# A softmax router on one core: TensorE's loop entered in the middle, and a new order of the last steps

## The chip, the core and the metric

The kernel runs on one core of a Trainium2 chip. The time is the device time of one execution in microseconds (us), the median of several runs. The profile's span is a little shorter than that time: it reaches from the first to the last instruction of one profiled execution. The engines are TensorE (PE, with its weight loads, PEld, listed apart), VectorE (DVE), ScalarE (ACT), GpSimd (POOL) and SyncE (SP).

## The reference

```python
batch, seq, dim = 16, 512, 1024
num_loras = 8
x: (16, 512, 1024) float32, router_weights: (1024, 8) float32

logits = np.matmul(x, router_weights)
exp_logits = np.exp(logits - np.max(logits, axis=-1, keepdims=True))
return (exp_logits / np.sum(exp_logits, axis=-1, keepdims=True)).astype(np.float32)
```

There are 8192 rows of 1024 numbers. Each row gives eight logits and a softmax over those eight. x is 33.6 MB, the result 0.26 MB: the kernel reads much and computes little.

## The kernel before

The 8192 rows are cut into 64 row blocks (J = 64) of 128 rows, one row to a partition. Block j is `xa[:, j, :]`. For each block TensorE turns the eight 128 x 128 pieces of x (so that the long dimension lies on the partitions), VectorE copies five of the turned pieces from PSUM to SBUF and ScalarE the other three, and TensorE multiplies them with the weights. The turned pieces lie in two sets of buffers, for even and for odd blocks. The softmax is done for groups of eight blocks on VectorE and ScalarE, and for the last three blocks (ALONE) apart.

```python
    LOADS = [4] * 13 + [2, 2, 2] + [1] * 5      # blocks in each load: all but the last block
    PIECES = [4, 2, 2]                          # the last block comes in three loads
    G, SKIP = 8, 3
    TRIPS = 31
    ALONE = 3
    NG = (J - ALONE + SKIP) // G
    starts = [max(0, G * g - SKIP) for g in range(NG)]
    ends = [G * (g + 1) - SKIP for g in range(NG)]
    DONE = ends[-2]
    # ...
    VN, SN = 5, 3                               # pieces copied by VectorE, by ScalarE
```

So the groups end with blocks 4, 12, ..., 60, and blocks 61, 62 and 63 stand alone. The first load goes through float32 and a cast on ScalarE; all others are issued by GpSimd in one sequence, and DMA writes them to SBUF as bfloat16:

```python
    for i, r in enumerate(LOADS):
        if i:
            nc.gpsimd.dma_start(
                out=xa[:, first[i]:first[i] + r, :], in_=x_rows[:, first[i]:first[i] + r, :]
            ).then_inc(s_ld[i], 16)
    # ... (at i == 2 the identity matrix and the filler are made)
    for i, n in enumerate(PIECES):
        c = slice(cols[i] * P, (cols[i] + n) * P)
        nc.gpsimd.dma_start(out=xa[:, J - 1, c], in_=x_rows[:, J - 1, c]).then_inc(s_z[i], 16)
```

SyncE tells TensorE what has landed. A product of block j waits for three counts on `s_c[j % 2]`: VectorE's copy, ScalarE's copy, and SyncE's count, which says that block j + 2 has landed. So the transposes of block j + 2, which come right behind, need no wait of their own. At the end SyncE issues the two stores:

```python
    for j in range(J - 2):
        sp.wait_ge(s_tv, j + 1)
        if j + 2 < LOADS[0]:
            sp.wait_ge(s_cast, j + 3)
        elif j + 2 in first:
            sp.wait_ge(s_ld[first.index(j + 2)], 16)
        sp.sem_inc(s_c[j % 2], 1)
    sp.wait_ge(s_z[0], 16)
    sp.wait_ge(s_out, NG - 1)
    sp.dma_start(out=out_rows[:, 0:DONE, :], in_=outv[:, 0:DONE, :]).then_inc(s_st[0], 16)
    sp.wait_ge(s_out, NG + 1)
    sp.dma_start(out=out_rows[:, DONE:J, :], in_=outv[:, DONE:J, :]).then_inc(s_st[1], 16)
```

TensorE's work is a loop of 31 trips, two blocks each. The addresses are kept in registers. `fill()` is a matmul on constant data that nobody reads: it keeps TensorE busy.

```python
    def multiply(b, dst, want=3):
        for c in range(KO):
            if c == 0:
                pe.wait_ge(s_c[b], want).then_inc(s_c[b], -want)
            # ... one 128x128 by 128x8 matmul
            if c == KO - 1:
                m.then_inc(s_p, 1)

    nc.br("rows_loop", engines=only_pe)
    with nc.body("rows_loop", valid_engines=only_pe):
        loop_turn(1)          # transposes of an odd block
        fill()
        fill()
        multiply(0, None)     # product of the even block before it
        loop_turn(0)          # transposes of the next even block
        multiply(1, None)
        pe.br_lt(r_x[0], left_of(TRIPS - 1), on_true="rows_loop", on_false="rows_done")
    nc.switch_bb("rows_done")

    # behind the loop: blocks 62 and 63
    turn_piece(0)             # waits for s_z[0], turns four pieces of block 63
    turn_piece(1)
    multiply((J - 2) % 2, alone[1], want=2)
    turn_piece(2)
    # ... product of block 63 in three parts, each behind the copy of its pieces
```

ScalarE and VectorE, with what they do last (`peak`, `diff`, `total`, `recip`, `scale` are the five VectorE steps of a group: maximum, subtraction, sum, reciprocal, product; `power` is ScalarE's exp between the second and the third; `low_alone` and `power_alone` are maximum and exp of one block that stands alone):

```python
    # ScalarE
    for j in range(J - 2):
        act_copy(j)
        if j == 1:
            cast(1)
        if j - 1 in ends[:-1]:
            power(ends.index(j - 1))
    power(NG - 1)
    power_alone(0)
    act_copy(J - 2)
    act.wait_ge(s_zt[0], 1)
    act.copy(xTz[0], z_bank[0]).then_inc(s_zc[0], 1)
    power_alone(1)
    power_alone(2)

    # VectorE
    # ... dve_copy(j) and the groups before the last, one step after each copy
    later = group(NG - 1)
    later.pop(0)()            # peak
    later.pop(0)()            # diff
    low_alone(0)
    dve_copy(J - 2)
    later.pop(0)()            # total
    dve_piece(1)
    dve_piece(2)
    low_alone(1)
    low_alone(2)
    for f in later:           # recip, scale
        f()
    dve.wait_ge(s_e3, ALONE)
    # ... sum, reciprocal and product of the blocks that stand alone
```

Of the kernel before, what the change touches and what calls it, by code (L numbers as in the profile page):

```python
# [11 lines left out]
def kernel(  # L12
# [6 lines left out]
    nc = tc.nc  # L19
    P = 128  # L20
    B, S, D = x.shape
    D2, N = router_weights.shape
# [3 lines left out]
    J = M // P  # L26
# [12 lines left out]

    LOADS = [4] * 13 + [2, 2, 2] + [1] * 5  # L40
    PIECES = [4, 2, 2]
    G, SKIP = 8, 3
    TRIPS = 31
    LOOP_T = 2 * TRIPS
    ALONE = 3
    NG = (J - ALONE + SKIP) // G
    starts = [max(0, G * g - SKIP) for g in range(NG)]
    ends = [G * (g + 1) - SKIP for g in range(NG)]
    DONE = ends[-2]
    assert sum(LOADS) == J - 1 and sum(PIECES) == KO and ends[-1] == J - ALONE  # L50
    VN, SN = 5, 3
# [20 lines left out]
    w_bf = sb("w_bf", [P, KO, N], bf16)  # L72
# [4 lines left out]
    xTz = [sb(f"xTz{i}", [P, n, P], bf16) for i, n in enumerate(PIECES)]  # L77
# [4 lines left out]
    inv = [sb(f"inv{i}", [P, G, 1], fp32) for i in range(2)]  # L82
    low = sb("low", [P, ALONE], fp32)
    ev3 = sb("ev3", [P, ALONE, N], fp32)
    sum3 = sb("sum3", [P, ALONE, 1], fp32)
    inv3 = sb("inv3", [P, ALONE, 1], fp32)


    LG_AT = 0x2000000
    lg = ps("lg", [P, 2, G, 64], fp32)  # L90
    ptv = [ps(f"ptv{i}", [P, 8, P], bf16) for i in range(2)]
    pts = [ps(f"pts{i}", [P, 8, P], bf16) for i in range(2)]
    spare = ps("spare", [P, 512], fp32)
    extra = ps("extra", [P, 8, 64], fp32)

    sem = tc.alloc_semaphore
# [4 lines left out]
    s_ld = [sem(f"s_ld{i}") for i in range(len(LOADS))]  # L101
    s_z = [sem(f"s_z{i}") for i in range(len(PIECES))]
    s_cast = sem("s_cast")
# [7 lines left out]
    s_tv = sem("s_tv")  # L111
    s_ts = sem("s_ts")
    s_c = [sem(f"s_c{i}") for i in range(2)]
    s_zt = [sem(f"s_zt{i}") for i in range(len(PIECES))]
    s_zc = [sem(f"s_zc{i}") for i in range(len(PIECES))]
    s_p = sem("s_p")
# [7 lines left out]
    first = [sum(LOADS[:i]) for i in range(len(LOADS))]  # L124
    cols = [sum(PIECES[:i]) for i in range(len(PIECES))]
# [19 lines left out]

    sp = nc.sync

    for j in range(J - 2):
        sp.wait_ge(s_tv, j + 1)
        if j + 2 < LOADS[0]:  # L150
            sp.wait_ge(s_cast, j + 3)
        elif j + 2 in first:
            sp.wait_ge(s_ld[first.index(j + 2)], 16)
        sp.sem_inc(s_c[j % 2], 1)
    sp.wait_ge(s_z[0], 16)
    sp.wait_ge(s_out, NG - 1)
    sp.dma_start(out=out_rows[:, 0:DONE, :], in_=outv[:, 0:DONE, :]).then_inc(s_st[0], 16)
# [19 lines left out]
    for i, n in enumerate(PIECES):  # L177
        c = slice(cols[i] * P, (cols[i] + n) * P)
# [5 lines left out]
    pe = nc.tensor  # L184
    r_x = [pe.alloc_register(f"rx{c}") for c in range(KO)]
# [22 lines left out]
    def loop_turn(b):  # L208

        for c in range(KO):  # L210
            t = again(
                turn_like,
                ins=(turn_like.ins[0], at([[J * D, P], [1, P]], xa, r_x[c])),
                outs=(pe.lower_ap(turn_ap(b, c), opt=False),),
            )
            if c == VN - 1:
                t.then_inc(s_tv, 1)
            if c == KO - 1:
                t.then_inc(s_ts, 1)
        pe.reg_add(r_l, r_l, 256)  # L220
        for c in range(KO):
            if c == KO // 2:
                pe.reg_alu(r_l, r_l, -4097, ALU.bitwise_and)
            pe.reg_add(r_x[c], r_x[c], D * 2)
# [7 lines left out]
                t.then_inc(s_ts, 1)  # L232
        return t

    def multiply(b, dst, want=3):

        for c in range(KO):
            if c == 0:
                pe.wait_ge(s_c[b], want).then_inc(s_c[b], -want)  # L239
            if dst is None:  # L240
                m = again(
                    mult_like,
                    ins=(
                        pe.lower_ap(w_bf[:, c, :], opt=False),
                        pe.lower_ap(chunk(b, c), opt=False, for_matmul_weights=True),
                    ),
                    outs=(at([[2 * G * 64, P], [1, N]], lg, r_l),),
                    start_tensor_calc=(c == 0),
                    stop_tensor_calc=(c == KO - 1),
                )  # L250
            else:
                m = pe.matmul(  # L252
                    dst, lhsT=chunk(b, c), rhs=w_bf[:, c, :],
                    start=(c == 0), stop=(c == KO - 1),
                )
            if c == KO - 1:
                m.then_inc(s_p, 1)

    def fill():
        return pe.matmul(spare, lhsT=filler[:, 0:P], rhs=filler, start=True, stop=True)  # L260
# [17 lines left out]
    def left_of(i):  # L278

        return X_AT + D * 2 * (2 * i + 3) + (P - 1) * 2  # L280

    only_pe = OrderedEngineSet([pe.engine])
    nc.br("rows_loop", engines=only_pe)
    with nc.body("rows_loop", valid_engines=only_pe):
        loop_turn(1)
        fill()
        fill()
        multiply(0, None)
        loop_turn(0)
        multiply(1, None)  # L290
        pe.br_lt(r_x[0], left_of(TRIPS - 1), on_true="rows_loop", on_false="rows_done")
    nc.switch_bb("rows_done")


    alone = [lg[:, NG % 2, 0, 0:N], extra[:, 0, 0:N], spare[:, 0:N]]
    z_bank = [pts[1][:, 0:PIECES[0], :], ptv[1][:, 0:PIECES[1], :], ptv[0][:, 0:PIECES[2], :]]
    Z_ORDER = (0, 1, 2)
    def turn_piece(i):
        pe.wait_ge(s_z[i], 16)
        for c in range(PIECES[i]):  # L300
            k = (cols[i] + c) * P
            t = pe.transpose(z_bank[i][:, c, :], xa[:, J - 1, k:k + P], identity)  # L302
        t.then_inc(s_zt[i], 1)

    turn_piece(0)
    turn_piece(1)
    multiply((J - 2) % 2, alone[1], want=2)
    turn_piece(2)
    todo = [(i, c) for i in Z_ORDER for c in range(PIECES[i])]
    for k, (i, c) in enumerate(todo):  # L310
        if c == 0:
            pe.wait_ge(s_zc[i], 1)
        m = pe.matmul(  # L313
            alone[2], lhsT=xTz[i][:, c, :], rhs=w_bf[:, cols[i] + c, :],
            start=(k == 0), stop=(k == KO - 1),
        )
    m.then_inc(s_p, 1)
# [14 lines left out]
    def power_alone(k):  # L332
        act.wait_ge(s_low, k + 1)
        act.activation(
            ev3[:, k, :], alone[k], func=Exp, bias=low[:, k:k + 1]
        ).then_inc(s_e3, 1)

    def act_copy(j):
        act.wait_ge(s_ts, j + 1)
        act.copy(xTs[j % 2], pts[j % 2][:, 0:SN, :]).then_inc(s_c[j % 2], 1)  # L340

    cast(0)
    for j in range(J - 2):
        act_copy(j)
        if j == 1:
            cast(1)
        if j - 1 in ends[:-1]:
            power(ends.index(j - 1))
    power(NG - 1)
    power_alone(0)  # L350
    act_copy(J - 2)
    act.wait_ge(s_zt[0], 1)
    act.copy(xTz[0], z_bank[0]).then_inc(s_zc[0], 1)
    power_alone(1)
    power_alone(2)


    dve = nc.vector
# [5 lines left out]
    def dve_copy(j):  # L364
        dve.wait_ge(s_tv, j + 1)
        dve.tensor_copy(out=xTv[j % 2], in_=ptv[j % 2][:, 0:VN, :]).then_inc(s_c[j % 2], 1)  # L366

    def group(g):
        b, n = g % 2, ends[g] - starts[g]
        rows = lg[:, b, G - n:G, 0:N]  # L370

        def peak():
            dve.wait_ge(s_p, ends[g])
            dve.reduce_max(mx[b][:, 0:n, 0], rows, axis=X).then_inc(s_d, 1)  # L374

        def diff():
            dve.wait_ge(s_d, 3 * g + 1)
            dve.tensor_tensor(  # L378
                out=ex[b][:, 0:n, :], in0=rows, in1=mx[b][:, 0:n, :].broadcast_to([P, n, N]),
                op=ALU.subtract,  # L380
            ).then_inc(s_ex, 1)

        def total():
            dve.wait_ge(s_ev, g + 1)
            dve.reduce_sum(ssum[b][:, 0:n, 0], ev[b][:, 0:n, :], axis=X).then_inc(s_d, 1)

        def recip():
            dve.wait_ge(s_d, 3 * g + 2)
            dve.reciprocal(inv[b][:, 0:n, :], ssum[b][:, 0:n, :]).then_inc(s_d, 1)  # L389

        def scale():
            dve.wait_ge(s_d, 3 * g + 3)
            dve.tensor_tensor(  # L393
                out=outv[:, starts[g]:ends[g], :], in0=ev[b][:, 0:n, :],
                in1=inv[b][:, 0:n, :].broadcast_to([P, n, N]), op=ALU.mult,
            ).then_inc(s_out, 1)

        return [peak, diff, total, recip, scale]

    def low_alone(k):  # L400
        dve.wait_ge(s_p, J - ALONE + k + 1)
        dve.reduce_max(  # L402
            low[:, k:k + 1], alone[k], axis=X, negate=True
        ).then_inc(s_low, 1)
# [3 lines left out]
        dve.tensor_copy(out=xTz[i], in_=z_bank[i]).then_inc(s_zc[i], 1)  # L408

    later = []  # L410
    for j in range(J - 2):
        dve_copy(j)
        if j in ends[:-1]:
            later += group(ends.index(j))
        if later:
            later.pop(0)()
    assert not later
    later = group(NG - 1)
    later.pop(0)()
    later.pop(0)()  # L420
    low_alone(0)
    dve_copy(J - 2)
    later.pop(0)()
    dve_piece(1)
    dve_piece(2)
    low_alone(1)
    low_alone(2)
    for f in later:
        f()
    dve.wait_ge(s_e3, ALONE)  # L430
    dve.reduce_sum(sum3[:, :, 0], ev3, axis=X).then_inc(s_d, 1)  # L431
    dve.wait_ge(s_d, 3 * (NG) + 1)
# [35 lines left out]
```

## Time and profile before

| what | before |
|---|---|
| device time, median of 3 | 87.9 us (87.88 to 87.9) |
| span of the profiled execution | 86.2 us |
| TensorE busy (matmuls) | 61.3 us, 71% |
| TensorE busy (weight loads) | 49.0 us, 57% |
| VectorE busy | 38.9 us, 45% |
| ScalarE busy | 37.9 us, 44% |
| GpSimd busy | 13.4 us, 16% |
| granted TensorE clock | 1.000 |

In the lines of the profile, "L273" is a line of the program. L260 is the line of the loop's products and of the fills, L273 that of the loop's transposes, L252 the product behind the loop, L302 the transposes of block 63, L313 its products, L366 and L340 the copies by VectorE and ScalarE, L408 and L353 those of block 63's pieces, L374 to L393 the group's softmax, L402 and L334 the maximum and exp of a block alone. A line of the timeline gives the start in us, the duration from first to last of the merged instructions in us, engine, operation, out<-in, count, and in brackets the idle time before and what ended it. Matmul ends are modelled, and a matmul overlaps the next. In a line of a window stand the window, its length, the busy time of PE, PEld, DVE, ACT and POOL (with counts), the granted clock, the busy share of the DMA engines, and the GB/s that they wrote. A line of waits names who waited for whom: us in total, times, longest.

### The profile page before, as it was taken

What the parts mean: (1) busy time and instruction counts of PE and PEld (TensorE: products, weight loads), DVE (VectorE), ACT (ScalarE), POOL (GpSimd) and SP (SyncE); (2) the same over time, 40 slices, a digit from 0 to 9 for tenths busy, and PEclk for the clock granted to TensorE, in tenths of its full rate; (3) what the DMA queues carried; (4) which work ended last, traced back from release to release, by engine and by line L of the source; (5) the groups of instructions that cost most, each with busy time, mean ns of one, the idle gap of its engine ahead of it and who ended that gap; (6) DMA issues with size and microseconds to landing.
All of it is one profiled execution on the core that took longest, in us unless ns stands there. A gap on an engine that the chain in (4) does not pass through costs nothing. (4 is left out here: it accounts for less than half of the span.)

```text
span 86.2 us, 2819 instructions
## 1 busy us (share of the span) xinstructions
PE 61.3 (71%) x1096; PEld 49.0 (57%) x1096; DVE 38.9 (45%) x113; ACT 37.9 (44%) x80; POOL 13.4 (16%) x30
## 2 busy tenths in 40 slices
PE   0051869999594949769493968859494999897940
PEld 0040827887482828466481837657381888675630
DVE  0020214676272634636172544726074557553652
ACT  0049396465262444526062443615154446544460
POOL 0489999700000000000000000000000000000000
PEclk9999999999999999999999999999999999999999
DMA  2999999999999999999999999999999999999720
GB/s 57 373 426 300 202 224 202 224 202 236 190 236 198 232 205 221 217 213 224 202 232 198 232 198 232 202 228 213 213 221 198 213 213 204 208 209 206 120 77 21
DMA packets 3906, 18.14 MB, mean 210 GB/s; under 512 B 568, under 2 KB 1080, under 8 KB 2112
## 3 DMA queue, kind: packets, MB, share of 16 engines
q0 software_dynamic: 3312, 15.73, 89.4%
q1 hardware_dynamic: 576, 2.36, 7.1%
q10 hardware_dynamic: 16, 0.03, 0.2%
q14 instruction: 2, 0.02, 0.0%
HBM read 33.59 MB, written 0.26 MB: 393 GB/s over the span
## 5 line engine op out<-in xcount | busy, mean ns | idle before, releaser
L366 DVE COPY xTv<-ptv 128x640 bf16<-128x640 bf16 x63 | 31.0, 492 | 36.3 <-PE ptv L273 32.1
L340 ACT COPY xTs<-pts 128x384 bf16<-128x384 bf16 x63 | 30.2, 479 | 38.9 <-PE pts L273 37.6
L273 PE MATMUL ptv<-identity,x_all 128*128 128x128 bf16 x311 | 27.9, 220 | 2.1 <-ACT x_all L325 2.1
L260 PEld LDWEIGHTS lg<-w_bf,xTv 128*128 128x128 bf16 x310 | 14.5, 96 | 25.1 <-issue 21.0
L260 PE MATMUL lg<-w_bf,xTv 128*128 128x8 bf16 x310 | 16.7, 167 | 14.0 <-PEq L239 13.8
L273 PE MATMUL pts<-identity,x_all 128*128 128x128 bf16 x186 | 20.7, 220 | 0.0
L273 PEld LDWEIGHTS ptv<-identity,x_all 128*128 (+1 forms) x311 | 18.2, 97 | 2.8 <-issue 2.6
L260 PE MATMUL spare<-filler 128*128 128x512 bf16 x63 | 19.5, 391 | 0.0
L260 PE MATMUL lg<-w_bf,xTs 128*128 128x8 bf16 x186 | 13.4, 166 | 0.0
L273 PEld LDWEIGHTS pts<-identity,x_all 128*128 x186 | 13.1, 99 | 0.0
L166 POOL DMA_DIRECT2D x_all<-in_x_dram x20 | 10.7, 612 | 2.8 <-POOLq L143 2.8
L260 PEld LDWEIGHTS lg<-w_bf,xTs 128*128 128x128 bf16 x186 | 9.0, 96 | 0.0
L260 PEld LDWEIGHTS spare<-filler 128*128 128x128 bf16 x63 | 5.0, 99 | 0.0
L267 PE MATMUL extra<-ident,w 8*128 8x8 f32 x8 | 1.0, 251 | 5.3 <-PEq L265 5.3
L325 ACT CAST x_all<-x_f 128x1024 bf16<-128x1024 f32 x4 | 4.0, 1044 | 0.0
L267 PEld LDWEIGHTS extra<-ident,w 8*128 8x128 f32 x8 | 0.9, 196 | 5.3 <-issue 5.3
L325 ACT ACT_TABLE_LOAD x1 | 1.3, 1283 | 5.5 <-ACTq L323 5.5
L360 DVE CAST identity<-ident 128x128 bf16<-128x128 f32 x1 | 0.5, 519 | 5.3 <-POOL ident L172 5.3
L374 DVE TENSOR_REDUCE mx<-lg 128x8 f32<-128x64 f32 (+1 forms) x8 | 1.8, 222 | 2.4 <-PE lg L260 2.4
L330 ACT ACTIVATE ev<-ex 128x64 f32<-128x64 f32 (+1 forms) x8 | 2.0, 254 | 0.8 <-DVE ex L378 0.7
L179 POOL DMA_DIRECT2D x_all<-in_x_dram x3 | 1.7, 696 | 0.0
L393 DVE TENSOR_TENSOR outv<-ev,inv 128x64 f32<-128x64 f32 (+1 forms) x8 | 1.7, 213 | 0.0
(36 smaller groups left out, 14.8 us busy)
## 6 DMA issues: line engine op xcount, KB each, us to landing
x_all<-in_x_dram POOLq DMA_DIRECT2D x12, 1024.0 KB, 32.1
x_f<-in_x_dram SPq DMA_DIRECT2D x2, 1024.0 KB, 6.2
x_all<-in_x_dram POOLq DMA_DIRECT2D x3, 512.0 KB, 60.1
x_all<-in_x_dram POOLq DMA_DIRECT2D x5, 256.0 KB, 64.2
out_dram<-outv SPq DMA_DIRECT2D x1, 212.0 KB, 1.9
x_all<-in_x_dram POOLq DMA_DIRECT2D x1, 128.0 KB, 65.8
x_all<-in_x_dram POOLq DMA_DIRECT2D x2, 64.0 KB, 65.6
out_dram<-outv SPq DMA_DIRECT2D x1, 44.0 KB, 1.5
```

What stands on the lines that cost most here:

```text
L166: nc.gpsimd.dma_start(out=xa[:, first[i]:first[i] + r, :], in_=x_rows[:, first[i]:first[i] + r, :]).then_inc(s_ld[i], 16)
L179: nc.gpsimd.dma_start(out=xa[:, J - 1, c], in_=x_rows[:, J - 1, c]).then_inc(s_z[i], 16)
L260: return pe.matmul(spare, lhsT=filler[:, 0:P], rhs=filler, start=True, stop=True)
L267: t = pe.transpose(w_ps[:, n, :], w8[:, :, n], ident[0:KO, 0:KO])
L273: turn_like = pe.transpose(turn_ap(0, 0), xa[:, 0, 0:P], identity).ins
L325: act.copy(xa[:, k, :], x_f32[:, k, :]).then_inc(s_cast, 1)
L330: act.activation(ev[g % 2][:, 0:n, :], ex[g % 2][:, 0:n, :], func=Exp).then_inc(s_ev, 1)
L340: act.copy(xTs[j % 2], pts[j % 2][:, 0:SN, :]).then_inc(s_c[j % 2], 1)
L360: dve.tensor_copy(out=identity, in_=ident).then_inc(s_idb, 1)
L366: dve.tensor_copy(out=xTv[j % 2], in_=ptv[j % 2][:, 0:VN, :]).then_inc(s_c[j % 2], 1)
L374: dve.reduce_max(mx[b][:, 0:n, 0], rows, axis=X).then_inc(s_d, 1)
L393: dve.tensor_tensor(out=outv[:, starts[g]:ends[g], :], in0=ev[b][:, 0:n, :], in1=inv[b][:, 0:n, :].broadcast_to([P, n, N]), op=ALU.mult,). ...
```

## The change

The loop's body is cut into two blocks, `rows_multiply` and `rows_turn`, and is entered at the second. Each trip now ends after the transposes of an even block, so that the last odd block's product (block 61) comes behind the loop with its own, fixed address. The fills move to just before the odd block's product. The product of an even block now waits for its two copies alone (want=2); a new count, `s_in`, tells TensorE that the next even block has landed, and it is waited for just before that block's transposes. Odd blocks keep the old wait (want=3). SyncE raises `s_in` for even blocks without waiting for TensorE first.

The groups end one block earlier (SKIP 4: they end with blocks 3, 11, ..., 59), and four blocks stand alone. The last steps of VectorE and ScalarE are put in a new order: the copies of blocks 61 and 62 come ahead of the exps of the blocks that stand alone, and the group's last steps are spread between the copies.

The purpose is that TensorE need not wait for data before a product which doesn't use it, and that little softmax work stands between the last blocks' landings and the last store.

```diff
-    G, SKIP = 8, 3
+    G, SKIP = 8, 4
-    ALONE = 3
+    ALONE = 4
+    s_in = sem("s_in")

-    for j in range(J - 2):
-        sp.wait_ge(s_tv, j + 1)
-        if j + 2 < LOADS[0]:
-            sp.wait_ge(s_cast, j + 3)
-        elif j + 2 in first:
-            sp.wait_ge(s_ld[first.index(j + 2)], 16)
-        sp.sem_inc(s_c[j % 2], 1)
+    for j in range(2, J - 1):
+        if j % 2:
+            sp.wait_ge(s_tv, j - 1)
+        if j < LOADS[0]:
+            sp.wait_ge(s_cast, j + 1)
+        elif j in first:
+            sp.wait_ge(s_ld[first.index(j)], 16)
+        sp.sem_inc(s_c[1] if j % 2 else s_in, 1)

-    def multiply(b, dst, want=3):
+    def multiply(b, dst, want=2):

-    nc.br("rows_loop", engines=only_pe)
-    with nc.body("rows_loop", valid_engines=only_pe):
-        loop_turn(1)
+    nc.br("rows_turn", engines=only_pe)
+    with nc.body("rows_multiply", valid_engines=only_pe):
         fill()
         fill()
+        multiply(1, None, want=3)
+        pe.br("rows_turn")
+    with nc.body("rows_turn", valid_engines=only_pe):
+        loop_turn(1)
         multiply(0, None)
+        pe.wait_ge(s_in, 1).then_inc(s_in, -1)
         loop_turn(0)
-        multiply(1, None)
-        pe.br_lt(r_x[0], left_of(TRIPS - 1), on_true="rows_loop", on_false="rows_done")
+        pe.br_lt(r_x[0], left_of(TRIPS - 1), on_true="rows_multiply", on_false="rows_done")

+    multiply((J - 3) % 2, alone[1])
     turn_piece(0)
     turn_piece(1)
-    multiply((J - 2) % 2, alone[1], want=2)
+    multiply((J - 2) % 2, alone[2])
     turn_piece(2)

     # ScalarE
-    for j in range(J - 2):
+    for j in range(J - 3):
         act_copy(j)
     # ...
     power(NG - 1)
-    power_alone(0)
+    act_copy(J - 3)
     act_copy(J - 2)
     act.wait_ge(s_zt[0], 1)
     act.copy(xTz[0], z_bank[0]).then_inc(s_zc[0], 1)
-    power_alone(1)
-    power_alone(2)
+    for k in range(ALONE):
+        power_alone(k)

     # VectorE
-    for j in range(J - 2):
+    for j in range(J - 3):
         dve_copy(j)
     # ...
-    later = group(NG - 1)
-    later.pop(0)()
-    later.pop(0)()
+    peak, diff, total, recip, scale = group(NG - 1)
+    peak()
+    diff()
+    dve_copy(J - 3)
+    total()
     low_alone(0)
     dve_copy(J - 2)
-    later.pop(0)()
+    recip()
+    low_alone(1)
     dve_piece(1)
     dve_piece(2)
-    low_alone(1)
     low_alone(2)
-    for f in later:
-        f()
+    low_alone(3)
+    scale()
```

(The buffers in which the four blocks alone have their logits are listed anew; that is left out here.)

More of the change, by code (lines that the diff above doesn't have):

```diff
@@ L282 @@
     only_pe = OrderedEngineSet([pe.engine])
-    nc.br("rows_loop", engines=only_pe)
-    with nc.body("rows_loop", valid_engines=only_pe):
-        loop_turn(1)
+    nc.br("rows_turn", engines=only_pe)
+    with nc.body("rows_multiply", valid_engines=only_pe):
         fill()
         fill()
+        multiply(1, None, want=3)
+        pe.br("rows_turn")
+    with nc.body("rows_turn", valid_engines=only_pe):
+        loop_turn(1)
         multiply(0, None)
+        pe.wait_ge(s_in, 1).then_inc(s_in, -1)
         loop_turn(0)
-        multiply(1, None)
-        pe.br_lt(r_x[0], left_of(TRIPS - 1), on_true="rows_loop", on_false="rows_done")
+        pe.br_lt(r_x[0], left_of(TRIPS - 1), on_true="rows_multiply", on_false="rows_done")
     nc.switch_bb("rows_done")
-    alone = [lg[:, NG % 2, 0, 0:N], extra[:, 0, 0:N], spare[:, 0:N]]
+    alone = [lg[:, NG % 2, 0, 0:N], extra[:, 0, 0:N], spare[:, 0:N], lg[:, 1 - NG % 2, 0, 0:N]]
     z_bank = [pts[1][:, 0:PIECES[0], :], ptv[1][:, 0:PIECES[1], :], ptv[0][:, 0:PIECES[2], :]]
@@ L313 @@
         m = pe.matmul(
-            alone[2], lhsT=xTz[i][:, c, :], rhs=w_bf[:, cols[i] + c, :],
+            alone[3], lhsT=xTz[i][:, c, :], rhs=w_bf[:, cols[i] + c, :],
             start=(k == 0), stop=(k == KO - 1),
```

## The prediction

> **What bounds the kernel now.** I read the page first, then SyncE's waits, then DMA in short windows around the end, then the last ten microseconds of the timeline. In the page, the rows of slices and of queues say what sets the pace:
>
> ```profile
> PE   0051869999594949769493968859494999897940
> ...
> DMA  2999999999999999999999999999999999999720
> ...
> q0 software_dynamic: 3312, 15.73, 89.4%
> ...
> HBM read 33.59 MB, written 0.26 MB: 393 GB/s over the span
> ```
>
> DMA is full from the second slice to the 37th, TensorE is not. The 33.6 MB of x come in at a fixed pace: every load is issued by GpSimd by 16.7 us, with no wait on any other engine, so no edit of the compute can move a landing. SyncE, which passes the landings on to TensorE, mostly waits for data:
>
> ```profile
> SPq L154 <- DMA x_all<-in_x_dram: 40.8, 15, 3.6
> SPq L154 <- PE ptv L273: 23.9, 30, 1.7
> ```
>
> In a burst one trip of TensorE's loop (two row blocks) takes 1.73 us (transposes of an even block start at 70.38 and again at 72.11). Four row blocks arrive in about 4.9 us (the waits after the fills end at 61.84 and 66.73), so two arrive in 2.44 us. TensorE has 0.7 us to spare per trip and is back to waiting for data by 74.08. What counts is therefore what lies behind the last loads. The windows of the end show them stop:
>
> ```profile
> 79.80:80.40 0.60, 0.60 (x8) 0.22 (x6) 0.49 (x1) 0.34 (x1) 0.00 (x0) 1.00 1.30 190
> 80.40:81.00 0.60, 0.60 (x17) 0.60 (x17) 0.23 (x1) 0.14 (x1) 0.00 (x0) 1.00 0.99 127
> 81.00:81.60 0.60, 0.60 (x18) 0.54 (x14) 0.43 (x3) 0.26 (x2) 0.00 (x0) 1.00 0.04 4
> ```
>
> The last number is GB/s: 127, then 4. The semaphores follow: the last one-block load is issued at 14.5 us and lands 65.7 us later, so block 62 is there at 80.2; the three pieces of block 63 are issued from 15.0 to 16.0 and land after 65.5 to 65.8 us, so at 80.8, about 81.2 and 81.6. But the span ends at 86.2. The 4.6 us in between are the tail, and the timeline shows who holds it up:
>
> ```profile
> 79.06 0.20 PEld L260 LDWEIGHTS lg<-w_bf,xTv 128*128 128x128 bf16 x5 [0.59 <-issue]
> ...
> 79.40 0.45 PE L273 MATMUL ptv<-identity,x_all 128*128 128x128 bf16 x5
> ...
> 79.86 0.59 PE L260 MATMUL spare<-filler 128*128 128x512 bf16 x2
> ...
> 80.34 0.20 PEld L260 LDWEIGHTS lg<-w_bf,xTv 128*128 128x128 bf16 x5 [0.38 <-issue]
> ...
> 80.57 0.44 PE L273 MATMUL ptv<-identity,x_all 128*128 128x128 bf16 x5
> ...
> 80.75 0.23 DVE L374 TENSOR_REDUCE mx<-lg 128x8 f32<-128x64 f32 x1 [0.36 <-PE lg L260]
> ...
> 81.48 0.48 DVE L366 COPY xTv<-ptv 128x640 bf16<-128x640 bf16 x1
> ...
> 81.76 0.47 ACT L340 COPY xTs<-pts 128x384 bf16<-128x384 bf16 x1
> ...
> 82.34 0.20 PEld L252 LDWEIGHTS extra<-w_bf,xTv 128*128 128x128 bf16 x5 [0.81 <-issue]
> ...
> 82.55 0.12 PEld L302 LDWEIGHTS ptv<-identity,x_all 128*128 128x128 bf16 x2
> ...
> 82.89 0.29 DVE L408 COPY xTz<-ptv 128x256 bf16<-128x256 bf16 x1 [0.60 <-PE ptv L302]
> ...
> 83.48 0.17 DVE L402 TENSOR_REDUCE low<-spare 128x1 f32<-128x8 f32 x1 [0.23 <-PE spare L313]
> ...
> 84.61 0.34 SPq L159 DMA_DIRECT2D out_dram<-outv  x1
> ```
>
> From above: product of block 59 (starts once block 61 has landed), transposes of block 61, the two fills, product of 60, transposes of 62 at 80.57. Then the copies of 62 out of PSUM at 81.48 and 81.76, late because VectorE and ScalarE first do the softmax of the last group. The 0.81 us in which TensorE then has nothing to do ends with those copies; only then come the product of 62 and the last piece's transposes at 82.55, a microsecond after that piece landed.
>
> [...] after a product that TensorE had waited for, the next transposes start 0.18 us after the start of its second part (76.73 to 76.91), against 0.08 us where TensorE's queue was full (62.61 to 62.69), so 0.1 us, and nothing when the queue is full. [...] here the exp at 81.59 lasts 0.27 and the next operation starts at 81.76, an overlap of 0.10, so each further exp adds about 0.17.
>
> **The change part by part.** (1) The loop. Order of work in a trip stays the same, cut elsewhere; the fills move from behind the odd block's transposes to behind the even block's. An even block's product no longer waits for the landing of the block two ahead; its transposes have that wait (s_in). Added per trip: one branch and one wait, about 0.1 us when visible, 31 times 0.1 = 3.1 us in all, but inside 31 times 0.7 us of spare time: zero on the path. At the end it matters. The product of 59 still waits for block 61 (79.06), and block 61's transposes stay at 79.40. The product of 60 follows directly, at 79.85 instead of 80.34. The transposes of 62 wait for their landing, 80.2 plus the 0.1 us of the hand-over by SyncE; with the 0.03 us from weight load to matmul they start at 80.36 instead of 80.57: 0.21 us earlier.
>
> (2) The groups end with block 59. VectorE's maximum needs the product of 59, over at 79.44, so it runs at 79.5 and not at 80.75, the subtraction at 79.75, ScalarE's exp at 80.0 to 80.25. All of it now lies in the wait for block 62. Block 61's copies come then (79.98 and 80.27), ready before TensorE wants them after 62's transposes. Its product goes at about 80.95 (before 81.01).
>
> (3) The copies of 62. VectorE can read 0.49 us after the first transpose starts (79.40 to 79.89 for block 61), ScalarE after 0.66 (79.40 to 80.06). Before: ready at 81.06 and 81.23, done at 81.48 and 81.76, so held up by 0.42 and 0.53 us. After: 80.36 + 0.49 = 80.85 and 80.36 + 0.66 = 81.02, with both engines free (VectorE is through with sum and the first maximum at about 80.9). ScalarE's, the later one, gains 81.76 - 81.02 = 0.74 us. The product of 62 follows 0.58 us behind it (81.76 to 82.34): 81.60.
>
> (4) From there the steps are those of before: pieces 0 and 1 are transposed before (landed at 80.8 and 81.2), last piece's transposes 0.21 later at 81.81 (landed at 81.6, so 0.2 us in hand), its copy at 82.89 - 0.74 = 82.15, the last maximum at 82.74, its exp, sum, reciprocal, product and the store's issue at 84.61 - 0.74 = 83.87. Piece 0's copy on ScalarE starts at 81.6 and ends at 82.2, in time for its four products.
>
> (5) Added behind it: one more maximum of 0.17 us (in VectorE's wait), one more exp of 0.17 us (ScalarE is through with the first three at about 82.9, as the last maximum ends), and 32 elements instead of 24 in the last three VectorE operations: the multiply of 64 took 0.23 and of 24 took 0.18 us, so 8 elements are 0.01 us, three times 0.03 us. The store carries 48 KB and not 44: from 1.9 us for 212 KB and 1.5 for 44, 0.01 us. Sum: -0.74 + 0.03 + 0.01 = -0.70 us, and 87.9 - 0.7 = 87.2 us.
>
> **Rivals.** (a) The loop becomes slower by its two branches, its extra wait and the shifted fills, and TensorE comes late to the last blocks. Against it: 0.7 us to spare in each trip. What can show is one branch of 0.1 us at the end: 87.3. [...] (b) The last piece's landing becomes the bound, since only 0.2 us are left: if it moves by 0.3 us, 0.1 us of the gain goes, 87.3. For it speaks that DMA shares grow towards the end (1.30 in a window). (c) The new order blocks an engine: VectorE's sum waits for the group's exp ahead of copy 62, and ScalarE's four exps all come after piece 0's copy. In my times the first has 0.6 us in hand, the second ends just in time; 0.2 us of queueing there makes 87.4. (d) Only the fills and the early product help, and the softmax's move is neutral, as ScalarE is loaded either way: -0.2 us, 87.7.
>
> **Range and chances.** If nothing behind the last transposes gets shorter, the gain is at most the distance from the last landing (81.6) to those transposes before (82.55): 0.95 us, so about 86.9 is the floor. With (b) to (d) there is still a gain, to 87.3 to 87.7. I take 87.2, range 86.9 to 87.6. Two per cent is 1.76 us: twice what the tail can give, so faster by 2% is nearly excluded (0.02). Slower by 2% needs a loop that loses over 0.7 us in each trip (0.03). Within 2%: 0.95.
>
> **What would show it.** Right: loads stop at the same 81 us; no fill between the transposes of 61 and the product of 60; transposes of 62 at 80.3 to 80.4; the last group's maximum near 79.5; copies of 62 at about 80.9 and 81.0; product of 62 near 81.6; last store issued near 83.9; span 85.5. Wrong: TensorE still busy with earlier blocks when block 62 lands (rival a), TensorE idle before the last piece's transposes (b), or a gap ended by VectorE's maxima or ScalarE's exps between the last product and the sum (c).

## The result and the profile after

The changed kernel takes 87.11 us (86.98 to 87.25, 4 runs) where before takes 87.9 (4 runs beside it): a ratio of 0.9904, 95% interval 0.9881 to 0.9927. In a second comparison (run 5 below) the same pair gave 0.988 (0.9857 to 0.9903), 87.06 against 88.17.

The same rows of the page, now of the changed kernel:

```profile
PE   0052639999998986959496895959597799999860
...
DMA  3899999999999999999999999999999999999920
...
q0 software_dynamic: 3312, 15.73, 89.9%
...
HBM read 33.59 MB, written 0.26 MB: 395 GB/s over the span
```

DMA has not changed in the body: it is full from the second slice on, the same bytes come in at the same pace (395 GB/s over the span, before 393). TensorE's row does differ in the first quarter, where its clock came up later (at 18.3 us, before at 11.7; see run 4): there the trace's records of the granted clock begin, at 1.0, and a matmul of a transpose takes 311 to 314 ns in the median ahead of that moment and 217 to 219 behind it. Ahead of it no clock is on record, and the page counts that as 1.000. SyncE still waits most for data, if less than before (35.1 us where it was 40.8). Its waits for TensorE's transposes are fewer (18 where there were 30), as the even blocks no longer have one, though longer in sum (29.0 us where it was 23.9):

```profile
SPq L157 <- DMA x_all<-in_x_dram: 35.1, 17, 3.0
SPq L157 <- PE ptv L276: 29.0, 18, 2.8
```

In the three windows at the end (last number: GB/s) the loads stop at the same place, a little later:

```profile
79.80:80.40 0.60, 0.44 (x13) 0.35 (x10) 0.56 (x3) 0.25 (x2) 0.00 (x0) 1.00 1.25 197
80.40:81.00 0.60, 0.48 (x8) 0.46 (x8) 0.34 (x4) 0.37 (x2) 0.00 (x0) 1.00 1.30 171
81.00:81.60 0.60, 0.59 (x16) 0.50 (x14) 0.60 (x3) 0.44 (x1) 0.00 (x0) 1.00 0.24 30
```

In the trace's record of landings the last piece of block 63 arrives at 81.69 us after the start of the span, before the change at 81.53. Over all profiled runs of this study it lies between 81.53 and 81.93, in either kernel, so this is scatter from run to run. The timeline of the tail, to be read beside that of before (lines have moved: L276 for L273, L263 for L260, L255 for L252, L348 and L374 for the copies, L416 and L361 for those of block 63):

```profile
79.22 0.20 PEld L263 LDWEIGHTS lg<-w_bf,xTv 128*128 128x128 bf16 x5 [0.42 <-issue]
...
79.45 0.44 PE L276 MATMUL ptv<-identity,x_all 128*128 128x128 bf16 x5
...
79.63 0.23 DVE L382 TENSOR_REDUCE mx<-lg 128x8 f32<-128x64 f32 x1 [0.65 <-PE lg L263]
...
79.84 0.23 PEld L263 LDWEIGHTS lg<-w_bf,xTv 128*128 128x128 bf16 x5
...
80.15 0.26 ACT L338 ACTIVATE ev<-ex 128x64 f32<-128x64 f32 x1 [1.02 <-DVE ex L386]
...
80.52 0.44 PE L276 MATMUL ptv<-identity,x_all 128*128 128x128 bf16 x5 [0.28 <-PEq L295]
...
80.99 0.49 DVE L374 COPY xTv<-ptv 128x640 bf16<-128x640 bf16 x1 [0.26 <-PE ptv L276]
...
81.16 0.48 ACT L348 COPY xTs<-pts 128x384 bf16<-128x384 bf16 x1 [0.39 <-PE pts L276]
...
81.75 0.20 PEld L255 LDWEIGHTS spare<-w_bf,xTv 128*128 128x128 bf16 x5
81.75 0.59 ACT L361 COPY xTz<-pts 128x512 bf16<-128x512 bf16 x1
...
81.96 0.12 PEld L309 LDWEIGHTS ptv<-identity,x_all 128*128 128x128 bf16 x2
...
82.89 0.17 DVE L410 TENSOR_REDUCE low<-lg 128x1 f32<-128x8 f32 x1 [0.23 <-PE lg L321]
...
84.04 0.34 SPq L162 DMA_DIRECT2D out_dram<-outv  x1
```

The two copies of block 62 now wait for its transposes (the brackets name PE). Before, the transposes were done and the copies stood behind the softmax of the last group. The 0.81 us in which TensorE stood idle ahead of block 62's product is gone. From the landing of the last piece to the issue of the last store it was 84.61 - 81.53 = 3.08 us and is now 84.04 - 81.69 = 2.35 us: 0.73 us less.

But the time has a second part. The span is shorter by 0.5 us only (86.2 to 85.7), as in this profile the loads ended 0.16 us later and the last store took 0.06 us longer from its issue to the end of the span. The device time of the same two executions is shorter by 0.95 (87.93 to 86.98). The rest is outside the span: 1.7 us before, 1.3 after. The experiments take the two parts apart.

### The profile page after: what moved, and what is told of

It is laid out like the page before. It is cut to its first block, busy times and chain, and to the rows that moved or that the text cites. A ratio compares the mean times of both kernels' runs of the same rounds, so it can differ in the third digit from the quotient of the medians.

```text
span 85.7 us, 2847 instructions
## 1 busy us (share of the span) xinstructions
PE 63.7 (74%) x1094; PEld 52.0 (61%) x1094; DVE 38.9 (45%) x114; ACT 38.1 (44%) x81; POOL 13.4 (16%) x30
## 3 DMA queue, kind: packets, MB, share of 16 engines
q1 hardware_dynamic: 576, 2.36, 7.3%
## 5 line engine op out<-in xcount | busy, mean ns | idle before, releaser
L348 ACT COPY xTs<-pts 128x384 bf16<-128x384 bf16 x63 | 30.2, 479 | 38.0 <-PE pts L276 36.7
L374 DVE COPY xTv<-ptv 128x640 bf16<-128x640 bf16 x63 | 31.0, 492 | 34.1 <-PE ptv L276 29.8
L276 PE MATMUL ptv<-identity,x_all 128*128 128x128 bf16 x311 | 28.7, 225 | 13.1 <-SPq L157 8.8
L276 PEld LDWEIGHTS ptv<-identity,x_all 128*128 (+1 forms) x311 | 18.9, 99 | 14.4 <-issue 14.3
L276 PE MATMUL pts<-identity,x_all 128*128 128x128 bf16 x186 | 21.3, 225 | 0.0
L263 PEld LDWEIGHTS lg<-w_bf,xTv 128*128 128x128 bf16 x305 | 15.6, 98 | 7.9 <-issue 1.5
L263 PE MATMUL spare<-filler 128*128 128x512 bf16 x61 | 19.5, 401 | 0.6
L263 PE MATMUL lg<-w_bf,xTv 128*128 128x8 bf16 x305 | 16.6, 167 | 0.0
L276 PEld LDWEIGHTS pts<-identity,x_all 128*128 x186 | 13.6, 101 | 0.0
L263 PE MATMUL lg<-w_bf,xTs 128*128 128x8 bf16 x183 | 13.2, 166 | 0.0
L263 PEld LDWEIGHTS lg<-w_bf,xTs 128*128 128x128 bf16 x183 | 8.9, 96 | 0.0
L263 PEld LDWEIGHTS spare<-filler 128*128 128x128 bf16 x61 | 4.5, 101 | 2.5 <-issue 2.5
L386 DVE TENSOR_TENSOR ex<-lg,mx 128x64 f32<-128x64 f32 (+1 forms) x8 | 1.7, 212 | 0.0
```

The costliest lines, as they stand in the source:

```text
L276: turn_like = pe.transpose(turn_ap(0, 0), xa[:, 0, 0:P], identity).ins
L386: dve.tensor_tensor(out=ex[b][:, 0:n, :], in0=rows, in1=mx[b][:, 0:n, :].broadcast_to([P, n, N]), op=ALU.subtract,).then_inc(s_ex, 1)
```

## The experiments

All are compared with the kernel before in runs on the same chip. "Tail" is from the landing of the last piece to the issue of the last store in the profiled run; "span" is the mean over the runs; "outside" is device time less span, the median over the runs. In the row of before, the tail is that of the profile read above, the rest is from the chip of runs 5 to 8. The kernel before had spans of 86.44 to 86.47 us on these chips and 1.74 to 1.80 us outside.

| run | ratio to before (95%) | tail, us | span, us | outside, us |
|---|---|---|---|---|
| before | 1 | 3.08 | 86.44 | 1.74 |
| 1 loop alone | 0.9943 (0.9930 to 0.9956) | 3.07 | 86.44 | 1.30 |
| 2 last steps alone | 0.9917 (0.9899 to 0.9936) | 2.56 | 85.95 | 1.50 |
| 3 three blocks alone | 0.9870 (0.9855 to 0.9884) | 2.35 | 85.78 | 1.31 |
| 4 fills back | 0.9895 (0.9867 to 0.9924) | 2.39 | 86.08 | 1.33 |
| 5 after, again | 0.9880 (0.9857 to 0.9903) | 2.37 | 85.78 | 1.33 |
| 6 before, TensorE's program longer | 1.0009 (0.9997 to 1.0021) | 3.09 | 86.44 | 1.79 |
| 7 pieces first | 0.9861 (0.9839 to 0.9884) | 2.19 | 85.56 | 1.32 |
| 8 more jumps | 0.9878 (0.9855 to 0.9900) | 2.37 | 85.72 | 1.35 |
| 9 before, GpSimd's program longer | 0.9996 (0.9978 to 1.0013) | 3.08 | 86.45 | 1.77 |
| 10 before, loop cut in two | 1.0018 (1.0001 to 1.0034) | 3.04 | 86.42 | 1.76 |
| 11 all pieces first | 0.9861 (0.9834 to 0.9888) | 2.18 | 85.57 | 1.32 |
| 12 no fills | 0.9984 (0.9963 to 1.0005) | 2.36 | 86.66 | 1.31 |

**1. The loop alone.** The new loop and SyncE's new sequence in the kernel before; the product of 61 comes behind the loop with its own address:

```diff
+    multiply((J - 3) % 2, alone[0])
     turn_piece(0)
     turn_piece(1)
```

> The new loop and its waits with the old groups (ending with block 60, three blocks alone) and the old order of the last steps. Theory: the loop alone brings the transposes of block 62 forward by some 0.2 us, but the copies of 62 still stand behind the group's softmax, whose first step needs the product of 60 (now at about 79.9 instead of 80.4) and the first maximum alone, which needs the product of 61. VectorE's copy of 62 then starts near 81.4 and ScalarE's near 81.7, so only about 0.1 us is gained: 87.8. Rival: the gain comes from TensorE no longer waiting, so this has most of it: 87.3 or less. Rival that the two branches cost: 88.0 or more.

The tail is as long as before, 3.07 us, and so is the span. The profile shows block 62 turned 0.17 us after its landing (80.50 to 80.67), as the new wait promises, but its copies are held up by the softmax as before:

```profile
80.67 0.44 PE L275 MATMUL ptv<-identity,x_all 128*128 128x128 bf16 x5 [0.31 <-PEq L294]
...
81.66 0.17 DVE L408 TENSOR_REDUCE low<-lg 128x1 f32<-128x8 f32 x1 [0.73 <-PE lg L254]
...
81.75 0.48 DVE L372 COPY xTv<-ptv 128x640 bf16<-128x640 bf16 x1
81.86 0.27 ACT L340 ACTIVATE ev<-lg,low 128x8 f32<-128x8 f32 x1 [0.65 <-DVE low L408]
82.03 0.47 ACT L346 COPY xTs<-pts 128x384 bf16<-128x384 bf16 x1
```

VectorE stood idle for 0.73 us for the product of 61, to take its maximum. For the last half microsecond of that, block 62's pieces lay ready (an estimate: after the change VectorE's copy started 0.47 us behind the first transpose, which makes about 81.15 here). On the tail the theory holds. Yet the time is 0.5 us below that of before, all of it outside the span: 1.30 us instead of 1.80. Neither theory had that.

**2. The last steps alone.** The old loop with the new groups and order (the lines are set against the changed kernel). Block 61's logits come from the loop here and share a bank with block 60's, so both maxima (and exps) wait for the second of them:

```diff
-        dve.wait_ge(s_p, J - ALONE + k + 1)
+        dve.wait_ge(s_p, J - ALONE + max(k, 1) + 1)
     # ... (ScalarE's wait in power_alone alike)
-    low_alone(0)
     dve_copy(J - 2)
     recip()
+    low_alone(0)
     low_alone(1)
```

> The old loop in one block with the old waits, with the new groups (ending with block 59, four alone) and the new order. Block 61's logits now come from the loop and lie in the same bank as block 60's, so both maxima wait for the product of 61 and stand behind the copies of 62. Theory: the copies of 62 start as soon as the block is transposed, 81.05 and 81.2 instead of 81.5 and 81.8: 0.5 us gained, 87.4, that is most of the gain but not all. Rival (the gain is the loop's): 87.8 or more.

The tail is 0.52 us shorter, the span 0.49: the expected half microsecond. Both copies follow the transposes at once:

```profile
80.94 0.44 PE L274 MATMUL ptv<-identity,x_all 128*128 128x128 bf16 x5
...
81.42 0.49 DVE L368 COPY xTv<-ptv 128x640 bf16<-128x640 bf16 x1 [0.54 <-PE ptv L274]
...
81.59 0.48 ACT L342 COPY xTs<-pts 128x384 bf16<-128x384 bf16 x1 [0.60 <-PE pts L274]
```

But block 62 had landed at 80.58 and is turned only at 80.94, behind the product of 60, which in the old loop waits for that landing itself (its first weight load came at 80.71). So the order is worth 0.52, the loop on top of it 0.21, and the loop without it 0.01: the loop's gain passes to the end only where nothing stands between the transposes and the copies.

**3. Three blocks alone.** As after the change, but the group ends with block 60 again, with the copies kept ahead:

```diff
-    G, SKIP = 8, 4
+    G, SKIP = 8, 3
-    ALONE = 4
+    ALONE = 3
     # VectorE (ScalarE alike: copy 61, group's exp, copy 62)
+    dve_copy(J - 3)
     peak()
     diff()
-    dve_copy(J - 3)
-    total()
-    low_alone(0)
     dve_copy(J - 2)
+    total()
+    low_alone(0)
     # ... (block 62's maximum and the group's reciprocal move behind block 63's copies)
```

> As after the change, but the groups end with block 60 again and three blocks stand alone; the copies of 61 and 62 are kept ahead as far as the order allows (copy 61, the group's maximum and subtraction, copy 62, then the rest). Theory: what counts is the copies' place in the order, not where the group ends. The group's maximum runs near 80.5, its exp near 81.0, both just ahead of the copies of 62: 87.1, as after the change, within 0.1. Rival: the group's end one block earlier is what makes room; the exp delays ScalarE's copy of 62 by 0.1 to 0.3: 87.3 to 87.4.

The tail is 2.35 us, that of the changed kernel within a hundredth. The earlier end of the groups is not what gains; the place of the copies in the order is.

**4. The fills back** behind the odd block's transposes:

```diff
-        fill()
-        fill()
         multiply(1, None, want=3)
     # ... (the jump to rows_turn)
         loop_turn(1)
+        fill()
+        fill()
         multiply(0, None)
```

> As after the change, with the two fills behind the odd block's transposes again, where they were before. After the change TensorE's clock came up at 18.3 us instead of 11.8, and it ran late behind the data until about 28 us. Theory: the fills' place decides when the clock comes up (near 12 us here), but that is hidden behind the loads. At the end the product of 60 moves behind the fills again, to about 80.4, and the transposes of 62 from 80.52 to about 80.65: 87.2, so 0.1 slower than after the change. Rival: the late clock costs something, so this is faster than after the change by 0.1 or more: 87.0 or less.

The tail is 2.39 us against 2.37 and 2.35, so they cost 0.02 to 0.04 us there, less than the 0.1 I had expected: block 62 is turned at 80.63, 0.17 us after its landing as without them. The longer span of the profiled run (86.6 us) comes from the last store, issued at 84.15 and there at 86.56. TensorE's clock came up at 12.6 us here. I had thought that the fills' place decides this moment. It does not: with the fills in their old place it was 11.7 us in the profile of before, but 18.1 in run 2 and 17.0 in run 9, where TensorE's program is that of before.

**5. The changed kernel again,** beside runs 6 to 8 (no edit).

> The changed kernel itself, on the same chip as the next three, for comparison. Expected: 0.990 of before; the span 0.6 to 0.7 us shorter than that of before, and the part of the time outside the span 1.3 us where before has 1.7 to 1.8.

So it is: span 85.78 against 86.44, 0.66 us less, and outside 1.33 against 1.74, 0.41 us less.

**6. Before, with a longer program on TensorE.** What is outside the span? With a window laid behind its end, the kernel before shows one DMA packet on the queue of instructions:

```profile
q14 instruction: 1, 0.01, 0.9%
```

It starts at 87.7 us, 1.5 us behind the end of the span. In the changed kernel, the window behind the span's end is empty (this one is of run 5):

```profile
DMA packets 0, 0.00 MB, mean 0 GB/s; under 512 B 0, under 2 KB 0, under 8 KB 0
```

TensorE's program is 186 instructions before and 205 after; the edit makes it 205 in the old kernel:

```diff
     pe.wait_ge(s_fill, 1)
+    for _ in range(38):
+        pe.wait_ge(s_id, 1)
```

> The kernel before with 38 more waits on a count that is long there, put where TensorE waits for the first cast anyway, so that TensorE's program is as long as after the change (205 instructions instead of 186). In the profile of before one 8 KB instruction fetch comes 1.5 us after the end of the span, in none of the others so far, and the time outside the span is 1.7 to 1.8 us where the new loop has 1.3. Theory: [...] the late fetch costs the 0.45 us: with the padding it is gone, the span stays that of before and the time drops by 0.4 to 0.5 us (0.995 of before). Rival: the late fetch belongs to another engine or is only a sign of something else: the time stays that of before within 0.1 us.

The rival holds: 1.0009, the late fetch is there, and 1.79 us are outside. The length of TensorE's program is not the reason.

**7. The pieces first.** The changed kernel's tail still has 2.35 us behind the last landing, and two products stand ahead of transposes that don't need them:

```diff
+    pe.wait_ge(s_c[(J - 3) % 2], 2)
+    turn_piece(0)
     multiply((J - 3) % 2, alone[1])
-    turn_piece(0)
     turn_piece(1)
+    pe.wait_ge(s_c[(J - 2) % 2], 2)
+    turn_piece(2)
     multiply((J - 2) % 2, alone[2])
-    turn_piece(2)
```

> After the change, with the first four pieces of block 63 turned ahead of the product of 61, and its last two ahead of the product of 62 (each behind the same wait for the copies that free its bank). After the change ScalarE's copy of the four pieces starts at 81.75 and VectorE's of the last two at 82.31, each behind a product of 0.2 us that nobody waits for. Theory: both copies come 0.2 us earlier and so does the end: 0.2 us less than after the change. Rival: TensorE now waits for a landing with a product behind it, or the maximum of 62 comes late and takes the place: within 0.05 us of after the change.

The tail is 2.19 us, 0.16 to 0.18 shorter than after the change, and the time 86.91 us against 87.06 on the same chip. ScalarE's copy of four pieces comes earlier, and VectorE's two copies run together:

```profile
81.58 0.59 ACT L363 COPY xTz<-pts 128x512 bf16<-128x512 bf16 x1
...
81.90 0.54 DVE L418 COPY xTz<-ptv 128x256 bf16<-128x256 bf16 x2
```

After the change these were 81.75 and 81.87 with 0.72 for both, with the landings the same within 0.01 us. This version is faster than before by 1.4%. It is also faster than the changed kernel: the two intervals in the table overlap, but all five of its runs (86.81 to 86.95 us) lie below all five of the changed kernel on the same chip (87.01 to 87.23).

**8. More jumps.** A third block in the loop:

```diff
         loop_turn(1)
+        pe.br("rows_even")
+    with nc.body("rows_even", valid_engines=only_pe):
         multiply(0, None)
```

> After the change, with the second block of the loop cut once more, so that each of the 31 trips has three jumps instead of two. Theory: a jump is hidden as long as TensorE has work queued, and is worth at most 0.1 us in the last trip: within 0.1 us of after the change. [...]

87.05 us against 87.06: 31 more jumps cost nothing that shows.

**9 and 10. Two more of before.** In run 9 GpSimd's program is one instruction longer (52, as in all kernels with two blocks), in run 10 the old loop is cut in two:

```diff
     # run 9
+    for _ in range(2):
+        nc.gpsimd.wait_ge(s_m, 1)
     nc.gpsimd.drain()
     # run 10
         multiply(0, None)
+        pe.br("rows_even")
+    with nc.body("rows_even", valid_engines=only_pe):
         loop_turn(0)
```

> The kernel before with two more waits on a count that is long there, in GpSimd's program ahead of its last instruction: one instruction more (52 instead of 51), as in every kernel with the loop in two blocks. Nothing on the way of the data changes. So far the part of the time outside the span was 1.6 to 1.9 us in 24 of 27 runs of before and in all runs with the padded TensorE program, and 1.3 us in all runs of kernels with two blocks. Theory: GpSimd's program length decides it; here the outside part is 1.3 us in all or nearly all runs, the span stays at 86.4, and the time is 0.995 of before. Rival: it goes with the loop's form or with the moment at which the engines end; then this is as before, 1.000.

> The kernel before with its loop cut in two blocks ahead of the even block's transposes, with one jump more per trip, and the order of work, the waits and the last steps untouched. Every engine but TensorE gets one more label in its program by it. Theory: the same as for the GpSimd padding, as GpSimd's program is 52 long here too: span 86.4, outside part 1.3 us, 0.995 of before. Rival: only an earlier end or another order of work does it: 1.000 of before.

Both theories fall: 0.9996 and 1.0018, 1.77 and 1.76 us outside, and the late fetch in both profiles. More runs show the form of it: what is outside is either near 1.3 us or between 1.6 and 1.9, with little between. Of the runs of before, 21 of 89 had the short form (none of 11 on the chip of runs 1 to 4, three of 27 on that of runs 5 to 8, 18 of 51 on that of runs 9 to 12); of run 6 none of 22, run 9 two of 14, run 10 three of 22, run 2 three of 6. Of the kernels with the new loop and SyncE's new sequence all 60 had it. Every profile with the long form has the late fetch (before and runs 6, 9 and 10), none with the short one. The cause stays open. SyncE's new sequence and TensorE's new order of waits always came together here and were not tried apart; nor did the old kernel have TensorE's and GpSimd's programs lengthened at once, to 205 and 52. Nor need it be the loop alone: run 2, with the old loop, had the short form in half of its six runs, before on that chip in none.

**11. All pieces first.** The second pair of pieces too:

```diff
     turn_piece(0)
+    turn_piece(1)
     multiply((J - 3) % 2, alone[1])
-    turn_piece(1)
     # VectorE
-    low_alone(1)
     dve_piece(1)
+    low_alone(1)
```

> As the run with the pieces first, with the second pair of pieces also turned ahead of the product of 61, and VectorE's copy of it ahead of the maximum of 61. There VectorE copied the two pairs back to back from 81.90 to 82.44, and the last pair had landed at 81.70. Theory: the second pair is copied near 81.75, the last near 82.05 and the end comes 0.1 us earlier than with the pieces first. Rival: TensorE waits for the second pair's landing (81.35) and the product of 61 and the last pair come later: no gain, or up to 0.1 us lost.

No gain: 2.18 us, 0.9861 again. The second pair is copied at 81.73 as expected, but the last pair's transposes start at 81.81, 0.10 us behind its landing (81.71), and its copy at 82.15, as in run 7 (82.14). The landing itself sets the end, and it did so in run 7 already: there the last pair had landed at 81.70 and its transposes started at 81.80.

**12. No fills** in the loop:

```diff
-        fill()
-        fill()
         multiply(1, None, want=3)
```

> After the change without the fills in the loop (their output is read by nobody). Theory: without them TensorE is idle for a larger part of each trip, its clock comes up later or falls back, [...] TensorE ends late: 89 us or more. Rival: the fills only take time: same as after the change.

Neither. The granted clock does fall back, to a mean of 0.874 in the profiled run and of 0.84 to 0.894 over all 20 (0.97 to 1.0 in nine runs of the changed kernel), in spells of 3.4 us or more, as its row on the page shows:

```profile
PEclk9999999999956998555999569985899759999997
```

A slow trip is longer than the 2.44 us in which its data come: in the profile after the change, ahead of 18.3 us, one took 2.99 us (transposes of an even block at 14.85 and at 17.84). But TensorE is back in time at the end, and the tail in the profile is 2.36 us, as with fills. The span is longer all the same, 86.66 us on average. In the profiled run the reason is the last store: it took 2.4 us to land and not 1.6. Fifteen of its sixteen counts were there by 85.73 us, the sixteenth at 86.62. Why one count was late there, and in the profile of run 4, stays open. All 20 runs without fills had spans of 86.2 to 87.3 us, where the changed kernel had 85.7 to 85.9; what made those longer that were not profiled is not shown.

## Why the prediction was right, and where it was not

- **DMA paces the body, so only the tail counts: right.** The loads end at 81.5 to 81.9 us in every kernel, even with TensorE at half clock for long stretches (run 12, mean granted clock 0.874) or with a third jump (run 8). (The first load is issued by SyncE and not by GpSimd, as I wrote of all; this plays no part at the end.)
- **The loop's additions are hidden: right.** 31 jumps more cost nothing (run 8: 87.05 us against 87.06), and TensorE was waiting for data again ahead of the product of 59 (0.42 us idle before 79.22), so rival (a) falls. One jump did not show even where I had counted 0.1 us (my estimate, from the 0.18 and 0.08 us between a product's second part and the next transposes in the profile of before): block 61's transposes started 0.07 us after the second part of the product of 59 (79.38 to 79.45), where with the old compare-and-branch between them it was 0.18 (79.22 to 79.40). I had left these transposes in their old place. They gained 0.11 us against their landing, but block 62's landing comes later, so it goes no further.
- **Block 62 turned 0.2 us earlier: right.** Foretold at 80.36 with its landing at 80.2; measured at 80.52 with the landing at 80.35. Run 4 showed that this comes from the wait's new place more than from the fills': with the fills back it is still 0.17 us behind the landing.
- **The softmax of the group out of the way, copies of 62 earlier by 0.74: right.** Foretold 80.85 and 81.02, measured 80.99 and 81.16, with all loads 0.16 us later. The group's maximum came at 79.63 (79.5), the product of 62 at 81.75 (81.60), the last piece's transposes at 81.96 (81.81), the last maximum at 82.89 (82.74), the store at 84.04 (83.87): each step is off by the loads' delay and next to nothing else. But the credit I gave to the earlier end of the groups was misplaced: run 3 has the same tail without it.
- **Rival (b), the last landing as the bound: not here, but close.** The transposes started 0.27 us behind it; in runs 7 and 11 it was 0.10, and there it is the bound.
- **Rival (c), a blocked engine: no.** ScalarE's copy of the first pieces ended at 82.34, and the products began at 82.39, but VectorE's copy of the last two ran until 82.59. The last two products started at 82.64, behind that copy, when the six before them had started by 82.54. So ScalarE's copy held nothing up, with some 0.1 us in hand.
- **Rival (d), the fills and the early product alone: no.** The loop without the new order gained 0.01 us of the tail (run 1).
- **The sum: a term was missing, and the closeness of 87.11 to 87.2 is in part luck.** I took the time to be the span plus a constant. It is not: the part outside went from 1.74 to 1.33 us (run 5). I foretold 0.70 us less. In run 5 the span shrank by 0.66 us, close to that, but the time fell by 1.11. In the first comparison the time fell by 0.79 only, though some 0.4 us of it lie outside the span there too. The span of the one profile of before was short (86.2 us; its loads ended at 81.53, earlier than in any other profile), while the four runs after had 85.8 on average, about 0.4 less and not 0.7. So the span missed the forecast by 0.3 us and the part outside by 0.4, in opposite directions.

## What to carry to other kernels

Where DMA sets the pace, find the last landing and follow the chain behind it: what was worth something there was the order of each engine's queue, and an early start of one step gained only where the next engine's queue had nothing older in front (the loop alone gained 0.01 us of the tail, the order alone 0.52, both 0.73). Compare times with spans before you put a difference of 0.5% down to the code: here 0.4 us of 1.1 lay outside of the span.

## What the runs showed of the hardware

- The device time holds 1.3 us or 1.6 to 1.9 us beyond the span, run by run, and in the profiles the longer form goes with an 8 KB instruction fetch some 1.5 us behind the span. Three edits of the old kernel did not remove it (1.76 to 1.79 us outside in runs 6, 9 and 10); all 60 runs of kernels with the new waits were free of it. What decides it is not shown.
- TensorE's clock came up (the trace's records of it begin, at 1.0) between 11.7 us (before) and 18.5 us (run 6), and at 17.0 us in run 9, with TensorE's program that of before. In the profile of before five transposes took 0.74 us until then and 0.44 after. In the profiles of runs 1, 2, 4 and 5 the clock also fell to half once, for 3.4 us between 43 and 53 us, with the fills in place (mean granted clock 0.967 to 0.98). The loads ended between 81.53 and 81.93 us in all of these profiles.
- One of the sixteen counts of a 48 KB store came 0.9 us behind the fifteen others in two of the profiles (runs 4 and 12): the store took 2.4 us to land there and 1.6 in the profile after the change.
